# A hybrid SSM and short-convolution layer: other parameter loads and transposes, an earlier scaling in the opening, and another order of the last tiles

## The chip, the cores and the metric

One Trainium2 chip, of which the kernel uses one core. The metric is the device time of one execution in microseconds; the kernel before took 429.47 us (median of three runs, 429.3 to 429.89).

## The reference

One decoder layer for 1024 tokens of width 1024, all in fp32. The input is normalised and projected to six parts of 512 columns; an S5 state-space mixer takes one of them, a gated convolution three, and a SiLU gate path has one for each mixer.

```python
def reference(x, norm_gain, w_in, ...):
    h = x
    xn = rmsnorm(h, norm_gain[l])                       # 1024 x 1024
    proj = jnp.einsum('bld,dc->blc', xn, w_in[l])       # 1024 x 3072
    # u_ssm, z_ssm, h_conv, b_conv, c_conv, z_conv: 512 columns each
    y_ssm = s5_mixer(u_ssm, ...) * jax.nn.silu(z_ssm)
    y_conv = short_conv_mixer(h_conv, b_conv, c_conv, conv_w[l]) * jax.nn.silu(z_conv)
    y = jnp.concatenate([y_ssm, y_conv], axis=-1)
    h = h + jnp.einsum('blc,cd->bld', y, w_out[l])
    return rmsnorm(h, final_norm_gain)

def s5_mixer(u, a_re, a_im, log_dt, b_re, b_im, c_re, c_im, d_skip, w_glu, b_glu):
    # 32 groups of 16 channels, 64 complex states each
    # a, dt -> discretised ab (exp, sin, cos); bb = q * b
    # s = scan over positions of s = ab * s + bb u;  y = Re(c s) + d u
    # y = gelu(y); y = y * sigmoid(y @ w_glu + b_glu)
```

In the reference b_re and b_im have the shape (group 32, state 64, channel 16), c_re and c_im (group 32, channel 16, state 64).

## The kernel before

Tokens are held as eight tiles of 128 rows, tile `i` with the tokens 8c + i. Each tile is normalised, transposed on PE (`turn`, tiles `ps_x`), and scaled by the gain into a high part `xh` in fp32r (`gain`, on ACT) and a low part `xl` (`rest`, on DVE). Every projection is the sum of three products, high by high, high by low and low by high, of 8 matmuls each, into one of the four PSUM banks of the pool `pmm`; `psm` has the other four.

The opening has its order on PE, ACT and DVE written out by hand, in the string `START` (line 33), under `tc.manual_schedule`. A word of it stands for a step: `s`, `n` are square and norm of a tile, `t`, `g`, `x` the transposes, `xh` and `xl` of a pair of tiles (0 to 3), `w` warming transposes, `W` and `L` the high and low parts of the weights. `u` and `U` are products of the SSM input: digits for blocks and then the quarter of the tokens, then which of the three products; `u` takes the blocks one after the other, `U` alternates between them. `k20` (`keep_u`) is ACT's copy of block 2, half 0, from PSUM to the tile `us`, which has two buffers, and four transfers of it to the scratch tensor `uscr` on SP's queue. `p0` to `p2` are `transpose_params`, `d` with a number so many steps of `discretise`, the DVE computation of the SSM parameters, and `C` three ACT copies that lay `craw` into `cb`.

In `cb`, rows 0 to 31 hold C by group (through `craw` and `C`), rows 32 to 63 B by group, loaded directly. `p1` and `p2` transpose it channel by channel, 32 transposes of 64x64 in four tiles `ps_cb`, and ACT lays the results out as `b1`, `b2`, `c1`, `c2` of 128 rows (state, real and imaginary) by 512 (group, channel).

All loads are issued on SP's queue, in program order in the opening: x, w, the small parameters, x again, then C and B, then the transfers of `uscr`.

After the opening the scheduler places the steps of the string `ORDER`: convolution blocks (`mm_h`, `mm_c`, `mm_b`, `mm_z`) with the SSM's steps between them (`ssm_prep` makes `vv`, `rr` and `ec` on DVE; `ssm_lags` multiplies `vv` in `ps_k`). Then come the GLU, the gate products `mm_zs`, and the output product as seven products of half-size operands for each of four pairs of row tiles. A pair has the accumulators `ow`, `oz`, `ox`; DVE adds them to the residual tiles `xr` (`xa` and `xb` for a pair), ACT takes squares with a sum (`sq`), and the root of the final norm is computed on DVE alone by an integer estimate and three Newton steps (`rsqrt_steps`, lines 88 to 99). In the last pair the last of the seven products is made in two halves of 256 columns, and GpSimd multiplies by the gain ahead of the root.

Of the kernel before, what the change touches and what calls it, by code (L numbers as in the profile page):

```python
# [30 lines left out]
EPS = 1e-6  # L31
WARM = (26, 8, 14)
START = ("s0 w0 n0 c s1 W0 n1 W1 w1 t0 L0 g0 L1 U010hl x0 u010x. W2 s2 s3 W3 L2 n23 u20hx u30hx t1 L3 g1 u230l. s4 x1 s5 n45 "
         "U01231h u01lx. k00 p0 u11lx. k10 t2 u21lx. k20 u31lx. k30 d12 g2 s6 x2 s7 C n67 d12 U01232h u01232l t3 g3 d8 x3 u01232x. "
         "U01233h u03l p1 p2 u03x. k01 u13lx. k11 d u23lx. k21 u33lx. k31")
ORDER = "p0 0 1 2 m0 q0 i0 3 p1 4 5 o0 6 m1 q1 i1 7 p2 8 o1 9 m2 q2 i2 10 p3 11 o2 m3 q3 i3 12 13 o3 14 15"
MAGIC = 12582912.0
# [20 lines left out]
def hybrid_kernel(ctx: ExitStack, tc, x, norm_gain, w_in, a_re, a_im, log_dt, b_re, b_im,  # L58
# [68 lines left out]
    par = tc.alloc_tile_pool(name="par", bufs=1)  # L127
    xpool = tc.alloc_tile_pool(name="xstage", bufs=8)

    cb = big.tile([2 * NG, 3 * S * H], F32, tag="cy", name="cb")  # L130
    cb = cb.rearrange("g (r p h) -> g r p h", h=H, r=3)
    craw = pst.tile([NG, 2, H, S], F32, name="craw")
    lam_r = pst.tile([NG, 2, 2, S], F32, name="lam_r")
    ldt = pst.tile([P, NG], F32, name="ldt")
    d_r = pst.tile([NG, H], F32, name="d_r")
# [34 lines left out]
    nc.sync.dma_start(rows, conv_w[0].rearrange("k (b p) -> (k b) p", p=P))  # L170
    nc.sync.dma_start(rowb, b_glu[0].rearrange("(b p) -> b p", p=P))
    load((4, 5, 6, 7))
    nc.sync.dma_start(craw[:, 0], c_re[0])
    nc.sync.dma_start(craw[:, 1], c_im[0])
    for k, src in enumerate((b_re, b_im, b_re)):
        nc.sync.dma_start(cb[NG:2 * NG, k], src[0])


    pw = pmm.tile([P, P], F32, tag="mm", name="ps_warm")
# [69 lines left out]
    lam = par.tile([P, 2, NG], F32, name="lam")  # L249
    c1 = par.tile([P, NG, H], F32, name="c1")  # L250
    c2 = par.tile([P, NG, H], F32, name="c2")
    b1 = pst.tile([P, NG, H], F32, name="b1")
    b2 = pst.tile([P, NG, H], F32, name="b2")
    dT = par.tile([H, NG], F32, name="dT")

    def transpose_params(part):
        if part == 0:
            ps = psm.tile([P, 2, NG], F32, tag="sm", name="ps_lam")
            for k in range(2):
                PE.transpose(ps[:, k], lam_r[:, k].rearrange("g d p -> g (d p)"), ident[0:NG, 0:NG])  # L260
            A.copy(lam, ps)
            ps = psm.tile([P, 16 + NG], F32, tag="sm", name="ps_rows")
            PE.transpose(ps[:, 0:12], rows, ident[0:12, 0:12])
            PE.transpose(ps[:, 12:16], rowb, ident[0:NB, 0:NB])
            PE.transpose(ps[0:H, 16:16 + NG], d_r, ident[0:NG, 0:NG])
            A.copy(cw, ps[:, 0:12])
            A.copy(bg, ps[:, 12:16])
            A.copy(dT, ps[0:H, 16:16 + NG])
            return
        off = part - 1  # L270
        for q in range(2):
            hs = slice(q * 8, q * 8 + 8)
            ps = psm.tile([P, 8, 2 * NG], F32, tag="sm", name=f"ps_cb{off}{q}")
            for h in range(8):
                PE.transpose(ps[:, h], cb[:, off:off + 2, :, 8 * q + h].rearrange("g r p -> g (r p)"), ident[0:2 * NG, 0:2 * NG])  # L275
# [146 lines left out]
    with tc.manual_schedule(engines={mybir.EngineType.PE, mybir.EngineType.Activation, mybir.EngineType.DVE}):  # L424
        for what in START.split():
# [4 lines left out]
                warm(WARM[n[0]])  # L430
            elif what[0] == "d":
                discretise(int(what[1:]) if what[1:] else None)
            elif what[0] == "C":
                for k in range(3):
                    A.copy(cb[0:NG, k], craw[:, k % 2].rearrange("g h p -> g p h"))
# [381 lines left out]
    def mult(ps, op_a, op_b, j, first, cols=slice(0, 512)):  # L817
        out_ = ps[:, 0:cols.stop - cols.start]
        for m, (p, q) in enumerate(((0, 0), (0, 1), (1, 0))):
            for k in range(NB):  # L820
                PE.matmul(out_, aq[op_a, j][:, p, k], bq[op_b, k][:, q, cols], start=first and m + k == 0,  # L821
                          stop=m == 2 and k == NB - 1, skip_group_check=True)
# [16 lines left out]
    def finish(j, m, parts):  # L839
# [4 lines left out]
        V.scalar_tensor_tensor(x, x, r, g2b, MUL, MUL)  # L844
        nc.sync.dma_start(out_ci[:, 2 * j + m, :], x)

    load_res(0)
    first_product(0)
    for j in pairs:
# [32 lines left out]
        Q.tensor_tensor(ga[:, hi_], xa[:, hi_], g2b[:, hi_], MUL)  # L882
        Q.tensor_tensor(gb[:, hi_], xb[:, hi_], g2b[:, hi_], MUL)
        Q.tensor_tensor(ga[:, lo_], xa[:, lo_], g2b[:, lo_], MUL)
        ops, r = rsqrt_steps([part[:, 0:1], part[:, 1:2]])
        for op in ops:
            op()
        A.activation(xa, ga, AF.Copy, scale=r)
        nc.sync.dma_start(out_ci[:, 2 * j, :], xa)
        steps, r = rsqrt_steps([part[:, 2:3], part[:, 3:4], part[:, 4:5]])  # L890
        for q in range(2):
            c = slice(q * 256, q * 256 + 256)
            mult(pw[j][:, c], "A22", "T4", j, False, c)
            add(xb[:, c], pw[j][:, c])
            final_square(xb[:, c], part[:, 3 + q:4 + q])
            Q.tensor_tensor(gb[:, c], xb[:, c], g2b[:, c], MUL)
# [4 lines left out]
        A.activation(xb[:, hi_], gb[:, hi_], AF.Copy, scale=r)
        for c in (lo_, hi_):
            nc.sync.dma_start(out_ci[:, 2 * j + 1, c], xb[:, c])
    ph3.release()
# [30 lines left out]
```

## Time and profile before

| what | value |
|---|---|
| median of three runs | 429.47 us (429.3, 429.89, 429.47) |
| profiled execution | 429.41 us, span 427.5 us, mean granted TensorE clock 0.990 |
| PE busy | 414.7 us, 97% of the span, 2226 instructions |
| DVE busy | 333.3 us, 78% |
| ACT busy | 183.5 us, 43% |
| transfers on SP's queue | 47712 packets, 45.42 MB |

The span runs from the first to the last instruction, and the execution is 1.9 us longer. PE is the engine that matmuls and transposes run on, PEld its weight loads, DVE the vector engine, ACT the scalar engine, POOL GpSimd, SP the queue that issues most transfers. "L230" is a line of the kernel. A row of the chain gives a start, a duration, and the work that the end of the program was waiting for at that time.

### The profile page before, as it was taken

What the parts mean: (1) busy time and instruction counts of PE and PEld (TensorE: products, weight loads), DVE (VectorE), ACT (ScalarE), POOL (GpSimd) and SP (SyncE); (2) the same over time, 40 slices, a digit from 0 to 9 for tenths busy, and PEclk for the clock granted to TensorE, in tenths of its full rate; (3) what the DMA queues carried; (4) which work ended last, traced back from release to release, by engine and by line L of the source; (5) the groups of instructions that cost most, each with busy time, mean ns of one, the idle gap of its engine ahead of it and who ended that gap; (6) DMA issues with size and microseconds to landing.
All of it is one profiled execution on the core that took longest, in us unless ns stands there. A gap on an engine that the chain in (4) does not pass through costs nothing.

```text
span 427.5 us, 6316 instructions
## 1 busy us (share of the span) xinstructions
PE 414.7 (97%) x2226; PEld 355.2 (83%) x2226; DVE 333.3 (78%) x820; ACT 183.5 (43%) x331; POOL 36.5 (9%) x41
## 2 busy tenths in 40 slices
PE   8898999999999999999999999999999999999992
PEld 7898999888888888888888888888888888888881
DVE  4973898969998999997997934867186799978634
ACT  4743944143423346135324413647335664333113
POOL 0000003000120020200022000120112100000022
PEclk9999998999999999999999999999999999999997
DMA  7892104514080361355025431677554550333212
GB/s 228 242 288 69 32 2 117 179 43 155 13 207 7 113 184 46 80 136 162 0 52 126 134 90 53 195 196 208 138 147 74 141 130 1 106 115 126 98 50 99
DMA packets 49472, 48.96 MB, mean 115 GB/s; under 512 B 6697, under 2 KB 39489, under 8 KB 49441
## 3 DMA queue, kind: packets, MB, share of 16 engines
q1 hardware_dynamic: 47712, 45.42, 35.7%
q0 software_dynamic: 1728, 3.15, 4.3%
q8 instruction: 17, 0.28, 0.3%
q14 instruction: 15, 0.11, 0.1%
HBM read 31.65 MB, written 8.39 MB: 94 GB/s over the span
## 4 chain that ended last, share of the span: by engine, by line
PE 94%; DMA 2%; DVE 1%; ACT 1%; issue 1%; SPq 1%; ACTq 0%
PE mm_u L230 11%; PE mm_b L230 10%; PE mm_c L230 10%; PE mm_h L230 10%; PE mm_z L230 10%; PE mm_zs L230 10%; PE ow L821 10%; PE glu L749 5%; PE oz L821 5%; PE ox L821 3%; DMA wru<-in_w_in_dram 2%; PE ps_s L571 2%; PE ps_y L595 2%; PE ps_y L596 2%; PE ps_x L211 1%; PE ps_cb L275 1%
## 5 line engine op out<-in xcount | busy, mean ns | idle before, releaser
L643 POOL TENSOR_TENSOR cy<-cy,sg 128x512 f32<-128x512 f32 x8 | 16.1, 2015 | 179.2 <-DVE sg L642 146.9
L828 ACT ACTIVATE sq<-xr 128x512 f32<-128x512 f32 (+1 forms) x17 | 10.3, 605 | 38.7 <-DVE xr L825 27.2
L749 PE MATMUL glu<-shl,wg 128*128 128x512 f32 x96 | 21.9, 389 | 0.0
L749 PEld LDWEIGHTS glu<-shl,wg 128*128 128x128 f32 x96 | 18.0, 188 | 3.7
L224 DVE SCALAR_TENSOR_TENSOR xl<-ps_x,g,xh 128x256 fp32r<-128x256 f32 x32 | 12.9, 476 | 8.6 <-ACT xh L218 8.6
L230 PE MATMUL mm_u<-xh,whu 128*128 128x256 f32 x128 | 17.5, 288 | 1.8 <-ACT xh L218 1.8
L230 PE MATMUL mm_u<-xh,wlu 128*128 128x256 f32 x128 | 18.6, 292 | 0.0
L230 PE MATMUL mm_u<-xl,whu 128*128 128x256 f32 x128 | 18.3, 293 | 0.0
L230 PEld LDWEIGHTS mm_u<-xh,whu 128*128 128x128 f32 x128 | 16.2, 191 | 2.5 <-ACT xh L218 2.2
L821 PE MATMUL ow<-bs,ax 128*128 128x512 f32 (+1 forms) x54 | 16.9, 367 | 0.5 <-DVE xr L825 0.5
L230 PEld LDWEIGHTS mm_u<-xh,wlu 128*128 128x128 f32 x128 | 17.1, 200 | 0.1
L230 PEld LDWEIGHTS mm_u<-xl,whu 128*128 128x128 f32 x128 | 17.0, 200 | 0.1
L230 PE MATMUL mm_b<-xh,whb 128*128 128x512 f32 x64 | 16.4, 398 | 0.0
L230 PE MATMUL mm_c<-xh,whc 128*128 128x512 f32 x64 | 16.1, 391 | 0.0
L230 PE MATMUL mm_h<-xh,whh 128*128 128x512 f32 x64 | 16.1, 391 | 0.0
L230 PE MATMUL mm_h<-xh,wlh 128*128 128x512 f32 x64 | 16.1, 390 | 0.0
L230 PE MATMUL mm_b<-xh,wlb 128*128 128x512 f32 x64 | 15.9, 391 | 0.0
L230 PE MATMUL mm_b<-xl,whb 128*128 128x512 f32 x64 | 15.8, 390 | 0.0
L230 PE MATMUL mm_h<-xl,whh 128*128 128x512 f32 x64 | 15.8, 389 | 0.0
L230 PE MATMUL mm_z<-xh,wlz 128*128 128x512 f32 x64 | 15.8, 389 | 0.0
L230 PE MATMUL mm_zs<-xh,whzs 128*128 128x512 f32 x64 | 15.8, 389 | 0.0
L230 PE MATMUL mm_zs<-xl,whzs 128*128 128x512 f32 x64 | 15.8, 389 | 0.0
(354 smaller groups left out, 1106.5 us busy)
## 6 DMA issues: line engine op xcount, KB each, us to landing
ee<-ec SPq DMA_DIRECT2D x16, 256.0 KB
wro<-in_w_out_dram SPq DMA_DIRECT2D x8, 512.0 KB
xr<-in_x_dram SPq DMA_DIRECT2D x8, 512.0 KB
out_dram<-xr SPq DMA_DIRECT2D x7, 512.0 KB
x<-in_x_dram SPq DMA_DIRECT2D x6, 512.0 KB
wrh<-in_w_in_dram SPq DMA_DIRECT2D x4, 512.0 KB
wrc<-in_w_in_dram SPq DMA_DIRECT2D x4, 512.0 KB
uscr<-us SPq DMA_DIRECT2D x32, 64.0 KB
```

The costliest lines, as they stand in the source:

```text
L211: PE.transpose(pss[kt // 2][:, kt % 2, j], x_t[2 * pair + j][:, kt * P:(kt + 1) * P], ident)
L224: V.scalar_tensor_tensor(xl[pair // 2][:, kt, n], ps, g1[:, kt:kt + 1], hs.bitcast(F32), MUL, SUB)
L230: PE.matmul(ps[:, n], a[:, kt], b[half][:, kt, n], start=what == "h" and kt == 0, stop=last and kt == KT - 1)
L275: PE.transpose(ps[:, h], cb[:, off:off + 2, :, 8 * q + h].rearrange("g r p -> g (r p)"), ident[0:2 * NG, 0:2 * NG])
L571: PE.matmul(ps[:, g - 4 * q], w1[:, g], u2[:, g], start=True, stop=True)
L595: PE.matmul(ps[:, k], tp[:, g], u2[:, g], start=True, stop=False)
L596: PE.matmul(ps[:, k, 1:C], vv[:, g, 1:T + 1].rearrange("p t h -> p (t h)"), xa[:, g, 0:C - 1], start=False, stop=True)
L643: Q.tensor_tensor(yb[:, n], yb[:, n], sg, MUL)
L749: PE.matmul(ps, wg[:, a, k, es], shl[half][:, y, k], start=m + k == 0, stop=m == 2 and k == NB - 1)
L821: PE.matmul(out_, aq[op_a, j][:, p, k], bq[op_b, k][:, q, cols], start=first and m + k == 0, stop=m == 2 and k == NB - 1, skip_group_check ...
L828: A.activation(temp(f"sq{final_square.n}")[:, 0:x.shape[-1]], x, AF.Square, accum_out=acc)
```

## The change

Four things change.

1. C is loaded three times (real, imaginary, real) in blocks of 128 rows (8 groups by 16 channels), so that 8 transposes of 128x128 in two tiles `ps_c` replace the 32. B goes from its tensor straight into `b1` and `b2`, by four transfers whose runs are the 16 channels of a group and state. The step `C` is gone; one ACT operation turns the signs of half of `b2`.
2. In `START`, `g2` stands ahead of `k20`, and the product `U01232h` of four blocks is split into `U012h`, blocks 0 and 1, and `U232h`, blocks 2 and 3.
3. The second half of the last product has a PSUM bank of its own, `ol`, and the order of the last pair's steps on ACT and DVE is written out by hand. The residual takes the part of the second half that is already in `ow` by an extra addition. The whole root of `xa` stands ahead of the last addition on DVE.
4. The root of `xb` is ACT's Sqrt, DVE's reciprocal and one Newton step. A Sqrt of one column of a scratch tile ahead of the first output product loads its table. The scaling of `xa` is split between DVE and ACT.

```diff
-START: ... k10 t2 u21lx. k20 u31lx. k30 d12 g2 s6 x2 s7 C n67 d12 U01232h u01232l t3 g3 d8 x3 u01232x. ...
+START: ... k10 t2 g2 u21lx. k20 u31lx. k30 d12 s6 x2 s7 n67 d12 U012h U232h u01232l t3 g3 d8 x3 u01232x. ...
...
-    nc.sync.dma_start(craw[:, 0], c_re[0])
-    nc.sync.dma_start(craw[:, 1], c_im[0])
-    for k, src in enumerate((b_re, b_im, b_re)):
-        nc.sync.dma_start(cb[NG:2 * NG, k], src[0])
+    for k, src in enumerate((c_re, c_im, c_re)):
+        nc.sync.dma_start(craw[:, :, k], src[0].rearrange("(b g) h p -> (g h) b p", g=G))
+    b1 = pst.tile([P, NG, H], F32, name="b1")
+    b2 = pst.tile([P, NG, H], F32, name="b2")
+    for dst, srcs in ((b1, (b_re, b_im)), (b2, (b_im, b_re))):
+        for k, src in enumerate(srcs):
+            nc.sync.dma_start(dst[k * S:k * S + S], src[0].rearrange("g p h -> p g h"))
...
-        for q in range(2):
-            hs = slice(q * 8, q * 8 + 8)
-            ps = psm.tile([P, 8, 2 * NG], F32, tag="sm", name=f"ps_cb{off}{q}")
-            for h in range(8):
-                PE.transpose(ps[:, h], cb[:, off:off + 2, :, 8 * q + h].rearrange("g r p -> g (r p)"), ident[0:2 * NG, 0:2 * NG])
-            for dst, lo, scale in (...):
-                A.activation(dst[:, :, hs], ps[:, :, lo:lo + NG].rearrange("p h g -> p g h"), AF.Copy, scale=scale)
+        ps = psm.tile([P, NB, P], F32, tag="sm", name=f"ps_c{off}")
+        for b in range(NB):
+            PE.transpose(ps[:, b], craw[:, b, off:off + 2].rearrange("q r p -> q (r p)"), ident)
+        dst, scale = ((c1, sgn), (c2, -1.0))[off]
+        A.activation(dst.rearrange("p (b g) h -> p b (g h)", b=NB), ps, AF.Copy, scale=scale)
+        if off:
+            A.activation(b2, b2, AF.Copy, scale=nsgn)
...
-            elif what[0] == "C":
-                for k in range(3):
-                    A.copy(cb[0:NG, k], craw[:, k % 2].rearrange("g h p -> g p h"))
...
+    A.activation(temp("root")[:, 0:1], ident[:, 0:1], AF.Sqrt)
     load_res(0)
     first_product(0)
...
-        ops, r = rsqrt_steps([part[:, 0:1], part[:, 1:2]])
-        for op in ops:
-            op()
-        A.activation(xa, ga, AF.Copy, scale=r)
+        ops, ra = rsqrt_steps([part[:, 0:1], part[:, 1:2]])
+        vh, v2, rb, t = (const.tile([P, 1], F32, name=f"last_{m}") for m in ("vh", "v2", "rb", "t"))
+        pl = psm.tile([P, 512], F32, tag="sm", name="ol")
+        with tc.manual_schedule(engines={mybir.EngineType.Activation, mybir.EngineType.DVE}):
+            add(xb[:, 256:512], pw[j][:, 256:512])
+            for q in range(2):
+                c = slice(q * 256, q * 256 + 256)
+                bank = pl if q else pw[j][:, c]
+                mult(bank, "A22", "T4", j, q == 1, c)
+                add(xb[:, c], bank[:, 0:256])
+                final_square(xb[:, c], part[:, 3 + q:4 + q])
+                Q.tensor_tensor(gb[:, c], xb[:, c], g2b[:, c], MUL)
+                if q == 0:
+                    for op in ops:
+                        op()
+                    V.tensor_scalar(vh, part[:, 2:3], 0.5 / D, 0.5 * EPS, MUL, ADD)
+                    V.scalar_tensor_tensor(vh, part[:, 3:4], 0.5 / D, vh, MUL, ADD)
+                    V.tensor_scalar(v2, vh, 2.0, None, MUL)
+            A.activation(t, part[:, 4:5], AF.Sqrt, scale=1.0 / D, bias=v2)
+            V.tensor_scalar_mul(xa[:, lo_], ga[:, lo_], ra)
+            V.scalar_tensor_tensor(vh, part[:, 4:5], 0.5 / D, vh, MUL, ADD)
+            A.activation(xa[:, hi_], ga[:, hi_], AF.Copy, scale=ra)
+            V.reciprocal(rb, t)
+            V.scalar_tensor_tensor(v2, rb, vh, rb, MUL, MUL)
+            V.scalar_tensor_tensor(rb, v2, 1.5, rb, SUB, MUL, reverse0=True)
+            V.tensor_scalar_mul(xb[:, lo_], gb[:, lo_], rb)
+            A.activation(xb[:, hi_], gb[:, hi_], AF.Copy, scale=rb)
         nc.sync.dma_start(out_ci[:, 2 * j, :], xa)
-        steps, r = rsqrt_steps([part[:, 2:3], part[:, 3:4], part[:, 4:5]])
-        for q in range(2):
...
-            steps.pop(0)()
-        for step_ in steps:
-            step_()
-        V.tensor_scalar_mul(xb[:, lo_], gb[:, lo_], r)
-        A.activation(xb[:, hi_], gb[:, hi_], AF.Copy, scale=r)
```

ACT in the opening, before, from k10's copy on (`mm_u` of a copy is the block's bank, `ps_x` the transposes of a pair, `x` a tile):

```order
L243 COPY us_596<-mm_u_306 128x512
L243 COPY us_638<-mm_u_400 128x512
L243 COPY us_660<-mm_u_417 128x512
L218 ACTIVATE xh_85<-ps_x_602,g_111 128x256 x2
L218 ACTIVATE xh_85<-ps_x_603,g_111 128x256 x2
L218 ACTIVATE xh_85<-ps_x_604,g_111 128x256 x2
L218 ACTIVATE xh_85<-ps_x_605,g_111 128x256 x2
L192 ACTIVATE ysb,ss_686<-x_118 128x1024
L192 ACTIVATE ysb,ss_696<-x_119 128x1024
L435 COPY cb<-craw 32x1024 x3
L218 ACTIVATE xh_85<-ps_x_805,g_111 128x256 x2
```

And after:

```order
L244 COPY us_597<-mm_u_307 128x512
L219 ACTIVATE xh_85<-ps_x_603,g_110 128x256 x2
L219 ACTIVATE xh_85<-ps_x_604,g_110 128x256 x2
L219 ACTIVATE xh_85<-ps_x_605,g_110 128x256 x2
L219 ACTIVATE xh_85<-ps_x_606,g_110 128x256 x2
L244 COPY us_647<-mm_u_401 128x512
L244 COPY us_669<-mm_u_418 128x512
L193 ACTIVATE ysb,ss_687<-x_117 128x1024
L193 ACTIVATE ysb,ss_697<-x_118 128x1024
L219 ACTIVATE xh_85<-ps_x_803,g_110 128x256 x2
```

The eight scalings of the third pair now stand ahead of the copies of blocks 2 and 3, and the fourth pair's follow the squares at once.

SP's queue after, from the last load of x to the second group of `uscr` transfers (before, five loads of 32x1024 stand in the place of the seven):

```order
L146 DMA x_118<-in_x_dram 128x1024
L172 DMA craw<-in_ssm_c_re_dram 128x4x64
L172 DMA craw<-in_ssm_c_im_dram 128x4x64
L172 DMA craw<-in_ssm_c_re_dram 128x4x64
L177 DMA b_147<-in_ssm_b_re_dram 64x32x16
L177 DMA b_147<-in_ssm_b_im_dram 64x32x16
L177 DMA b_148<-in_ssm_b_im_dram 64x32x16
L177 DMA b_148<-in_ssm_b_re_dram 64x32x16
L246 DMA uscr<-us_564 8x16x128 x4
L246 DMA uscr<-us_597 8x16x128 x4
```

The seven loads stand ahead of every transfer that empties a buffer of `us`.

DVE at the end after, from the last addition of a whole bank on (`xr_3719` is xa, `xr_3721` xb, `ssp` the sums of squares, `y_3951` the root of xa; the rows of the second and third Newton step are cut):

```order
L821 TENSOR_TENSOR xr_3719<-xr_3719,ox_3875 128x512
L821 TENSOR_TENSOR xr_3721<-xr_3721,ow_3830 128x256
L92 TENSOR_SCALAR vh_3950<-ssp_3873 128x1
L94 SCALAR_TENSOR_TENSOR vh_3950<-ssp_3873,vh_3950 128x1
L95 TENSOR_SCALAR y_3951<-vh_3950 128x1
...
L899 TENSOR_SCALAR last_v_3954<-last_vh 128x1
L821 TENSOR_TENSOR xr_3721<-xr_3721,ol 128x256
L902 TENSOR_SCALAR xr_3719<-ysb,y_3951 128x512
L903 SCALAR_TENSOR_TENSOR last_vh<-ssp_3873,last_vh 128x1
L905 RECIPROCAL last_rb<-last_t 128x1
```

Before, the last addition from `ow` stands behind eight of the root's steps of xa and one of xb's, and eight steps of xb's root follow it.

More of the change, by code (lines that the diff above doesn't have):

```diff
@@ L33 @@
 START = ("s0 w0 n0 c s1 W0 n1 W1 w1 t0 L0 g0 L1 U010hl x0 u010x. W2 s2 s3 W3 L2 n23 u20hx u30hx t1 L3 g1 u230l. s4 x1 s5 n45 "
-         "U01231h u01lx. k00 p0 u11lx. k10 t2 u21lx. k20 u31lx. k30 d12 g2 s6 x2 s7 C n67 d12 U01232h u01232l t3 g3 d8 x3 u01232x. "
+         "U01231h u01lx. k00 p0 u11lx. k10 t2 g2 u21lx. k20 u31lx. k30 d12 s6 x2 s7 n67 d12 U012h U232h u01232l t3 g3 d8 x3 u01232x. "
          "U01233h u03l p1 p2 u03x. k01 u13lx. k11 d u23lx. k21 u33lx. k31")
@@ L128, in hybrid_kernel @@
     xpool = tc.alloc_tile_pool(name="xstage", bufs=8)
-    cb = big.tile([2 * NG, 3 * S * H], F32, tag="cy", name="cb")
-    cb = cb.rearrange("g (r p h) -> g r p h", h=H, r=3)
-    craw = pst.tile([NG, 2, H, S], F32, name="craw")
+    craw = pst.tile([P, NB, 3, S], F32, name="craw")
     lam_r = pst.tile([NG, 2, 2, S], F32, name="lam_r")
@@ L251, in hybrid_kernel @@
     c2 = par.tile([P, NG, H], F32, name="c2")
-    b1 = pst.tile([P, NG, H], F32, name="b1")
-    b2 = pst.tile([P, NG, H], F32, name="b2")
     dT = par.tile([H, NG], F32, name="dT")
@@ L270, in transpose_params @@
         off = part - 1
-        for q in range(2):
-            hs = slice(q * 8, q * 8 + 8)
-            ps = psm.tile([P, 8, 2 * NG], F32, tag="sm", name=f"ps_cb{off}{q}")
-            for h in range(8):
-                PE.transpose(ps[:, h], cb[:, off:off + 2, :, 8 * q + h].rearrange("g r p -> g (r p)"), ident[0:2 * NG, 0:2 * NG])
-            for dst, lo, scale in ((b2 if off else b1, NG, nsgn if off else 1.0), (c2 if off else c1, 0, -1.0 if off else sgn)):
-                A.activation(dst[:, :, hs], ps[:, :, lo:lo + NG].rearrange("p h g -> p g h"), AF.Copy, scale=scale)
+        ps = psm.tile([P, NB, P], F32, tag="sm", name=f"ps_c{off}")
[5 more added lines that the diff above has]
+            A.activation(b2, b2, AF.Copy, scale=nsgn)
     steps = []
@@ L884, in hybrid_kernel @@
         Q.tensor_tensor(ga[:, lo_], xa[:, lo_], g2b[:, lo_], MUL)
-        ops, r = rsqrt_steps([part[:, 0:1], part[:, 1:2]])
-        for op in ops:
-            op()
-        A.activation(xa, ga, AF.Copy, scale=r)
-        nc.sync.dma_start(out_ci[:, 2 * j, :], xa)
-        steps, r = rsqrt_steps([part[:, 2:3], part[:, 3:4], part[:, 4:5]])
-        for q in range(2):
[L892 to L896, printed above, removed]
-            steps.pop(0)()
```

## The prediction

> **What bounds the kernel now.** I read the busy table and the chain of work on the page first, since they say which engine a saving must come from.
>
> ```profile
> PE 414.7 (97%) x2226; PEld 355.2 (83%) x2226; DVE 333.3 (78%) x820; ACT 183.5 (43%) x331; POOL 36.5 (9%) x41
> PE 94%; DMA 2%; DVE 1%; ACT 1%; issue 1%; SPq 1%; ACTq 0%
> ```
>
> PE holds 94% of the chain, so an edit pays only where PE loses instructions, clock or a wait, or behind PE's last product. The waits of PE tell how much idle time there is to win.
>
> ```profile
> PE mm_u L230 <- ACT xh L218: 1.8, 2, 1.1
> PE ow L821 <- DVE xr L825: 0.5, 1, 0.5
> ```
>
> Next the chain in order of time (start, us, what), for the places that the change touches.
>
> ```profile
> 35.23 1.75 PE ps_x L211 x16
> ...
> 40.88 0.58 ACT us L243
> ...
> 41.90 7.94 PE mm_u L230 x64
> ...
> 51.59 8.63 PE mm_u L230 x72
> 60.22 3.66 PE ps_cb L275 x32
> 63.88 8.41 PE mm_u L230 x56
> 72.29 5.47 PE mm_h L230 x24
> ```
>
> Between 40.9 and 41.9 the chain leaves PE for ACT. The parameter transposes ps_cb take 3.66 us, and the 56 products behind them take 8.41 us, or 0.150 each, where the 72 ahead took 8.63, or 0.120. The stretches (columns: busy us, then the granted clock, DMA share, GB/s) say why:
>
> ```profile
> 63.00:64.00 1.00, 1.00 (x9) 0.93 (x9) 0.86 (x6) 0.83 (x3) 0.00 (x0) 0.93 0.00 0
> 64.00:65.00 1.00, 1.00 (x5) 1.00 (x6) 0.83 (x6) 0.67 (x2) 0.00 (x0) 0.50 0.00 0
> ...
> 67.00:68.00 1.00, 1.00 (x9) 1.00 (x9) 1.00 (x1) 0.44 (x1) 0.00 (x0) 0.86 0.00 0
> ```
>
> PE was granted half its clock from just before 64 to past 67, right behind ps_cb.
>
> **The opening, part by part.** *Transposes.* 32 transposes of 64x128 become 8 of 128x128. A 128x128 transpose takes 1.75/16 = 0.109 us in the ps_x row, so 8 take 0.88: **-2.78 us**, all on PE's path.
>
> *Clock.* The 56 products at 0.120 would take 6.72: the slow stretch cost 1.69. The 16 transposes of ps_x at 35.23 (1.75 us) show no such loss behind them, 0.120 per product. The new block of 0.88 is half of that block, so I take the drop as gone: **-1.69**; kept, it is worth 0.
>
> *The third pair's high parts.* In the timeline, with ACT's wait order:
>
> ```profile
> 41.37 3.03 ACT L218 ACTIVATE xh<-ps_x,g 128x256 fp32r<-128x256 f32 x8
> 41.90 4.10 PE L230 MATMUL mm_u<-xh,whu 128*128 128x256 f32 x32 [1.09 <-ACT xh L218]
> 46.52 5.95 ACT L435 COPY cb<-craw 32x1024 f32<-32x1024 f32 x3
> 33.38 11.11 SPq L245 DMA_DIRECT2D uscr<-us  x16
> ```
>
> The eight scalings start only when k30's copy has been made, and that waits for block 3's last product at 40.88. Put ahead of k20, they start behind ps_x (end 36.98) and take 3.03: ready by about 40.1, before PE's 40.81. k20 then runs at about 40.1 to 40.7 and k30 at 40.9 to 41.5. Blocks 2 and 3 of the next product need the banks that these two free; PE gets there after 16 products of 0.120, at 42.8, so 1.3 us are spare. **-1.09**.
>
> ACT loses the three C copies (5.95), and its eight parameter evictions become two of 128x512 and a scaling of b2; it is idle over half the time, so this pays only through what ACT hands to DVE.
>
> *Loads.* Five loads of 32 rows become three of 128x4 runs of 256 B (1536 packets) and four of 64x32 runs of 64 B, 8192 packets in all, or 512 for each of 16 DMA engines. They sit in SP's queue between x and the uscr writes of `us`. `us` has two buffers, so k20 waits until k00's four writes have landed, k30 for k10's. The loads begin where the five begin now, near 28:
>
> ```profile
> 26.00:28.00 2.00, 2.00 (x19) 2.00 (x18) 2.00 (x6) 2.00 (x6) 0.00 (x0) 1.00 1.11 406
> 28.00:30.00 2.00, 2.00 (x19) 2.00 (x18) 0.97 (x7) 1.66 (x4) 0.00 (x0) 1.00 1.01 197
> 36.00:40.00 4.00, 4.00 (x36) 4.00 (x35) 0.00 (x0) 0.59 (x1) 0.00 (x0) 1.00 0.37 98
> 17.50:17.75 0.25, 0.25 (x4) 0.25 (x3) 0.25 (x1) 0.25 (x1) 0.00 (x0) 1.00 0.23 45
> q1 hardware_dynamic: 47712, 45.42, 35.7%
> ```
>
> No row has 64-B reads alone. Bounds per packet and engine: low, the 128-B load of log_dt at 17.5: 45 GB/s for 0.25 us are 88 packets, 0.23 x 0.25 us on 16 engines, 10 ns. High, the mean of the queue, 35.7% of 16 x 427.5 us over 47712 packets of 952 B: 51 ns. Between them, w's 512-B runs at 406 GB/s (20 ns) and the uscr writes of 512 B (98 GB/s at share 0.37: 31 ns). I take 15: these are reads like w's, with an eighth of the bytes, so nearest to the 128-B row. With 96 packets of C (2 us) the loads end at 30 + 7.7 = 37.7; k00's and k10's writes (64 packets at 31 ns, 2 us) end by 39.7, and with some 1.5 us to land (an estimate from the tail row below: data until 426, end 427.5) k10's are there by 41.2, k30's 40.9 nearly kept. **0**, up to about 17 ns; each further ns costs 0.5 us.
>
> The Trainium skill, "DMA: Bandwidth & Descriptors", Specifications, speaks against this edit: transfers under 512 B are read, modified and written. By that rule a 64-B packet would cost no less than a 512-B one, and the sum would lose the 0 for what the rival below has. The 128-B row at 10 ns contradicts it so far.
>
> Sum to the end of the opening: -2.78 - 1.69 - 1.09 = **-5.56**.
>
> **What is late next: DVE.** DVE computes the SSM parameters beside PE's convolution blocks, and rows of the timeline and the chain show how close it is:
>
> ```profile
> 52.37 2.95 ACT L218 ACTIVATE xh<-ps_x,g 128x256 fp32r<-128x256 f32 x8
> 66.98 1.23 DVE L106 TENSOR_TENSOR wlh<-wrh,whh 128x1024 fp32r<-128x1024 f32 x1 [0.77 <-ACT whh L105]
> 77.44 1.23 DVE L106 TENSOR_TENSOR wlz<-wrz,whz 128x1024 fp32r<-128x1024 f32 x1 [0.59 <-ACT whz L105]
> 88.86 0.92 ACT L288 ACTIVATE rotc<-rot 64x112 f32<-64x112 f32 x3 [10.48 <-DVE rot L288]
> 95.50 0.68 DVE L620 TENSOR_TENSOR vp<-hs,mm_c 128x512 f32<-128x512 f32 x1
> 103.76 1.35 DVE L505 TENSOR_TENSOR vv<-vv,tv 128x1152 f32<-128x1152 f32 x1
> 105.83 0.32 PE ps_k L546 x2
> 95.00:105.00 10.00, 10.00 (x46) 8.23 (x46) 9.96 (x13) 2.44 (x3) 0.00 (x0) 1.00 0.63 193
> ```
>
> vv ends at 105.11, 0.7 before ps_k reads it, and DVE is busy 9.96 of 10 us there. DVE's chain starts earlier too, but not by 5.56. Its gate is the fourth pair's high parts, which start at 52.37, when the C copies (46.52 + 5.95) are done. Without the copies PE's transposes set that start: they end at 51.59 now, 50.5 when 1.09 earlier, and the scalings begin on their first banks, near 49.4: 3.0 sooner. DVE has some 0.6 of its own steps to do first, so 2.4; its waits on weight casts further on (0.77 and 0.59 in the rows) go too, as ACT has the casts ready earlier: 3.7 in all, an estimate, so that rot's end at 88.9 moves to about 85. vv is then ready at 101.4, PE at 100.2: **+1.2** given back. Bounds: 0 (DVE gains enough) and +2.5 (it gains 2.4 and no more).
>
> **The root's table.** Sqrt on a scratch column between the casts at 343 to 346 adds one table load, 1.28 us by its row, and a column's operation on ACT. Casts there run back to back at 0.52 each; PE's first product needs the first of them only, ACT gets the rest back within the first pair. **0**; with no cover, +1.3 once. Behind it only squares, copies and Sqrt follow.
>
> ```profile
> 97.71 1.28 ACT L641 ACT_TABLE_LOAD   x1
> ```
>
> **The tail.**
>
> ```profile
> 417.31 0.42 DVE xr L825
> ...
> 419.90 0.24 ACT xr L888
> ...
> 420.95 0.50 ACT sq L828 x2
> 421.48 0.17 DVE vh L94
> ...
> 423.21 0.72 ACT xr L901
> 423.80 0.81 SPq L903 DMA_DIRECT2D out_dram<-xr  x2
> 425.00:426.00 1.00, 0.00 (x0) 0.00 (x0) 0.00 (x0) 0.00 (x0) 0.00 (x0) 0.50 0.99 381
> ```
>
> The second half of the last product no longer waits for DVE's read of the bank: PE ends 0.5 earlier, about 418.9. But DVE now does all nine root steps of xa and three more ahead of the last add; at 0.216 each (the eight from 421.48 to 423.21 are 1.73) plus independence, they end near 420.1, 0.45 later than now. The square no longer stands behind xa's scaling of 1.15 us, so it ends near 421.1, 0.4 earlier. Then one Sqrt (about 0.3), reciprocal (0.3) and two steps (0.43) replace eight: scales at 422.2 instead of 423.2. xa's scaling, however, now stands behind the Sqrt on ACT and ahead of xb's: xa's transfer is issued near 422.2, not 421.1, and the three outputs of 1 MB run together. 512 KB take 1.35 us at 381 GB/s: 0.8 from issue to data (423.8 to 424.6), 2.7 of data, 1.5 to land: 427.15. **-0.35**; bounds 0.9 worse (the table must be loaded here: 1.28 - 0.35) and 1.2 better (outputs not serial).
>
> **Sum:** -5.56 + 1.2 - 0.35 = -4.7. The profiled execution took 429.41 (span 427.5, 1.9 around it), 0.06 under the median of 429.47; the forecast is **424.8**. Of the likeliest case alone the range is 423.3 to 426.0.
>
> **Rivals.**
>
> *B's loads hold up k20 (the other side).* If a 64-B packet takes 24 ns or more, the loads end at 30 + 12.3 or later, k10's writes have landed 3.5 after that, k30's copy ends near 46.4 and PE, due at 42.8, stalls some 3.5 in the split product; at 31 ns the loads end at 45.9, the stall is 7.1: -4.7 + 7.1 = +2.4, and an idle stretch of that length may bring another 1.69 of half clock: 432 to 434. At 51 ns it is 442. It decides from about 26 ns (the 4.7 gone). For it: the uscr row's 31. Against: 10 ns for 128 B. The skill's page named above gives this rival; its rule as a mechanism (a read before each write, two passes at 20 ns) means 40 ns, 512 x 40 = 20.5, loads end at 50.5: 437. Chance 0.15 in all, 0.04 of it for 40 ns and more.
>
> *Part of this stall,* 17 to 24 ns, costing 0.5 to 3.5: 425.3 to 428.5. Chance 0.17.
>
> *DVE keeps more:* its chain moves 2.4 only and the SSM blocks run at DVE's pace: -5.56 + 2.5 - 0.35 = -3.4, 426.1. For it: 9.96 of 10 busy. Against: the waits of PE name DVE nowhere in that stage. Chance 0.13.
>
> *DVE keeps nothing and the tail pays:* -5.56 - 0.35 to -1.2: 422.7 to 423.5. Chance 0.12.
>
> *The clock drop stays* (it was some other thing than the length of the transposes): -3.0, 426.4. Chance 0.07.
>
> **How the numbers follow.** The forecast's case has 0.36. 0.2% (0.86 us) is about what a measurement tells from no change. Slower: the first rival's upper part, 0.15; same: its threshold and the partial stall's end, 0.06; faster: 0.79. Leaving out some 0.14 above and 0.06 below, the range is 423.0 to 429.3.
>
> **What would show it.** ps_c at 0.88 and clock 1.00 behind it; no wait of PE on xh near 41; k20's copy at about 40, or named as waiting on a transfer; a wait of PE at ps_k on vv of about 1; three output transfers issued within 1.2 us. A wait of PE at the split product, or DMA share high past 40, makes the forecast wrong.

## The result and the profile after

The changed kernel took 426.81 us (median of six runs, 425.42 to 427.51), the kernel before 429.28 in the same comparison: ratio 0.9949, 95% interval 0.9932 to 0.9966, or 2.5 us of gain. The forecast was 424.8, 4.7 us of gain, almost twice what came. The direction held, and the wide range of 423.0 to 429.3; the range of the likeliest case, 423.3 to 426.0, did not. Against the larger sets of the kernel before that stand beside the experiments (429.17, 428.57 and 429.04) the gain is 1.8 to 2.4 us. One execution of the kernel before in the first of these sets took 697.69 us at a granted clock of 0.557, and the ratios leave it out.

The profiled execution has a span of 424.7 us, against 427.5. The page's busy table and chain:

```profile
PE 410.9 (97%) x2202; PEld 350.8 (83%) x2202; DVE 334.7 (79%) x819; ACT 177.6 (42%) x326; POOL 35.8 (8%) x41
PE 80%; DVE 11%; ACT 2%; DMA 2%; issue 2%; SPq 1%; ACTq 0%; DVEq 0%
```

PE has 3.8 us less to do, and its share of the chain fell from 94% to 80%: DVE now carries 11% of it. The waits of PE say the same. The wait of 0.5 at the end is gone, as is one of the two on xh; four new ones are there; the wait on xh that is left is the first product's.

```profile
PE ps_k L542 <- DVE vv L501: 0.8, 1, 0.8
PE mm_c L231 <- DVE vp L616: 0.7, 1, 0.7
PE mm_u L231 <- ACT xh L219: 0.7, 1, 0.7
PE mm_b L231 <- ACT us L244: 0.6, 1, 0.6
PE mm_u L231 <- ACT us L244: 0.4, 1, 0.4
```

A ledger by place needs a common zero. The first product of the opening starts once the first x has been loaded and scaled, at 12.1 to 13.0 us in the profiles of this study, in no order that goes with the edit, so every time below is counted from it. These are PE's rows of the timeline for the kernel before (start, duration, the first matmul, the first of mm_h, of ps_k, of the output product):

```profile
12.98 1.23 PE L230 MATMUL mm_u<-xh,whu 128*128 128x256 f32 x6 [0.71 <-ACT xh L218]
72.12 2.00 PE L230 MATMUL mm_h<-xh,whh 128*128 128x512 f32 x8
105.76 0.39 PE L546 MATMUL ps_k<-vv,bb 128*16 128x128 f32 x2
342.12 0.39 PE L821 MATMUL ow<-bd,bs 128*128 128x512 f32 x1
```

and for the changed kernel:

```profile
12.38 1.84 PE L231 MATMUL mm_u<-xh,whu 128*128 128x256 f32 x9 [0.67 <-ACT xh L219]
66.33 2.00 PE L231 MATMUL mm_h<-xh,whh 128*128 128x512 f32 x8
102.70 0.39 PE L542 MATMUL ps_k<-vv,bb 128*16 128x128 f32 x2 [0.76 <-DVE vv L501]
339.37 0.39 PE L817 MATMUL ow<-bd,bs 128*128 128x512 f32 x1
```

| from the first product to | before | after | difference |
|---|---|---|---|
| mm_h (end of the opening) | 59.14 | 53.95 | -5.19 |
| ps_k | 92.78 | 90.32 | -2.46 |
| the output product | 329.14 | 326.99 | -2.15 |
| the end of the span | 414.52 | 412.32 | -2.20 |

The opening gained 5.2 us. Of these, 2.7 were given back on the 36 us up to ps_k and 0.3 more between ps_k and the output product; the piece from the first output product to the end, all four pairs and the tail, took 85.33 instead of 85.38. The 0.60 by which the first product came earlier is the rest of the difference in span.

Why DVE is late shows in ACT's timeline of the changed kernel (copies k20 and k30, the squares s6 and s7) and in DVE's first step behind the first square:

```profile
39.69 0.58 ACT L244 COPY us<-mm_u 128x512 f32<-128x512 f32 x1 [0.88 <-DMA uscr<-us]
42.00 0.58 ACT L244 COPY us<-mm_u 128x512 f32<-128x512 f32 x1 [1.72 <-DMA uscr<-us]
42.48 1.06 ACT L193 ACTIVATE ysb<-x 128x1024 f32<-128x1024 f32 x1
43.66 1.06 ACT L193 ACTIVATE ysb<-x 128x1024 f32<-128x1024 f32 x1
43.66 0.15 DVE L92 TENSOR_SCALAR vh<-ss 128x1 f32<-128x1 f32 x1 [3.78 <-ACT ysb L193]
```

ACT stands still for 1.72 us ahead of k30 until the uscr transfers have landed. The squares of the last two tiles stand behind it on ACT, the norm of those tiles on DVE behind the squares, and the steps of discretise behind the norm; DVE idles 3.78 us. SP's queue tells what held the transfers:

```profile
24.70 1.44 SPq L172 DMA_DIRECT2D craw<-in_ssm_c_re_dram  x1
26.19 0.74 SPq L177 DMA_DIRECT2D b<-in_ssm_b_re_dram  x1
26.97 6.08 SPq L177 DMA_DIRECT2D b<-in_ssm_b_im_dram  x2
33.10 1.31 SPq L177 DMA_DIRECT2D b<-in_ssm_b_re_dram  x1
34.50 10.71 SPq L246 DMA_DIRECT2D uscr<-us  x16
```

The four loads of B hold SP from 26.19 to 34.41, and the first uscr transfer, whose data were ready at 32.8, is issued at 34.50, 1.7 late. In the kernel before, the last load of B was this one, and the first uscr transfer was issued at 33.38, when its data were ready:

```profile
24.75 0.42 SPq L176 DMA_DIRECT2D cb<-in_ssm_b_re_dram  x1
```

### The profile page after: what moved, and what is told of

Same layout as the page of the kernel before. It is cut to its first block, busy times and chain, and to the rows that moved or that the text cites. A ratio compares the mean times of both kernels' runs of the same rounds, so it can differ in the third digit from the quotient of the medians.

```text
span 424.7 us, 6263 instructions
## 1 busy us (share of the span) xinstructions
PE 410.9 (97%) x2202; PEld 350.8 (83%) x2202; DVE 334.7 (79%) x819; ACT 177.6 (42%) x326; POOL 35.8 (8%) x41
## 4 chain that ended last, share of the span: by engine, by line
PE 80%; DVE 11%; ACT 2%; DMA 2%; issue 2%; SPq 1%; ACTq 0%; DVEq 0%
PE mm_zs L231 10%; PE ow L817 10%; PE mm_b L231 9%; PE mm_z L231 9%; PE mm_c L231 8%; PE mm_h L231 8%; PE mm_u L231 6%; PE oz L817 5%; PE glu L745 5%; PE ox L817 3%; DVE e L287 2%; PE ps_s L567 2%; DMA wru<-in_w_in_dram 2%; PE ps_y L591 2%; PE ps_y L592 2%
## 5 line engine op out<-in xcount | busy, mean ns | idle before, releaser
L639 POOL TENSOR_TENSOR cy<-cy,sg 128x512 f32<-128x512 f32 x8 | 15.2, 1904 | 180.3 <-DVE sg L638 180.3
L219 ACT ACTIVATE xh<-ps_x,g 128x256 fp32r<-128x256 f32 x32 | 12.1, 489 | 8.9 <-PE ps_x L212 8.9
L231 PE MATMUL mm_c<-xl,whc 128*128 128x512 f32 x64 | 15.8, 389 | 0.0
```

Of the source, the lines that this page charges most:

```text
L219: A.activation(xh[pair // 2][:, kt, n], ps, AF.Copy, scale=g1[:, kt:kt + 1])
L231: PE.matmul(ps[:, n], a[:, kt], b[half][:, kt, n], start=what == "h" and kt == 0, stop=last and kt == KT - 1)
L639: Q.tensor_tensor(yb[:, n], yb[:, n], sg, MUL)
```

## The experiments

Theory A: the missing gain was lost on DVE, because B's loads hold SP's queue, that holds k20 and k30, and these hold the squares and DVE's whole chain. Its main rival is the prediction's own account, in which the fourth pair's high parts set DVE's time. The first four kernels ran beside one set of runs of the kernel before (median 429.17), the next four beside another (428.57), the last four beside a third (429.04).

**Four buffers of us.**

```diff
-        us = xw.tile([P, 4, C], F32, tag="us", name=f"us{b}{half}", bufs=2)
+        us = xw.tile([P, 4, C], F32, tag="us", name=f"us{b}{half}", bufs=4)
```

> The tile us has four buffers instead of two, so ACT's copies k20 and k30 wait for no transfer of uscr; the loads of B stay where they are. Theory A (the missing gain was lost because B's loads hold SP's queue, which holds k20 and k30, and with them the squares s6, s7 behind them on ACT and the whole DVE chain): k30 ends near 40.8 instead of 42.6, the squares end 1.7 us earlier, DVE's chain at vv moves by about 1.7, PE's wait in the split product (0.4) goes and its three waits on vp, us and vv (2.0 in all) shrink to under 0.7; total 1.3 to 2.0 us below the changed kernel's 426.8, so 424.8 to 425.5. Rival B (DVE's chain is bound by the fourth pair's high parts and its own work, as the prediction had it): only the 0.4 goes, and DVE gives it back; total 426.4 to 426.8, waits on vp, us and vv unchanged or larger.

425.89 us, ratio 0.9929 (0.9913 to 0.9945); 0.9 below the changed kernel, less than theory A said and more than the rival. The place is as theory A had it:

```profile
39.98 0.59 ACT L244 COPY us<-mm_u 128x512 f32<-128x512 f32 x1 [0.98 <-PE mm_u L231]
41.65 0.15 DVE L92 TENSOR_SCALAR vh<-ss 128x1 f32<-128x1 f32 x1 [2.06 <-ACT ysb L193]
99.31 1.35 DVE L501 TENSOR_TENSOR vv<-vv,tv 128x1152 f32<-128x1152 f32 x1
```

k30 now waits for PE alone. Counted from the first product, vv's last step starts at 87.22 instead of 88.92 (101.30 - 12.38), and ps_k at 88.62 instead of 90.32: 1.70 each. The wait at ps_k stays at 0.8, since PE came earlier too. Of the 1.70, 1.2 were left at the output product, where a wait of 0.4 of mm_zs on ACT (`sgl`) was new in this execution, and the piece from there to the end took 86.00 instead of 85.33.

This profile also tells the two gates apart. The page's chain of the changed kernel leads to DVE through the fourth pair's high parts, as the rival has it:

```profile
49.66 1.94 ACT xh L219 x5
```

But DVE's timeline has no idle time ahead of the low parts that follow them. With four buffers the high parts start only 0.62 earlier (36.66 instead of 37.28 after the first product), DVE's step behind the second square 1.73 earlier (30.74 instead of 32.47), and vv moved with the squares. One thing is not as firm: in the six profiles with two buffers and B's loads ahead of the transfers (the changed kernel and five below) k30 starts 28.58 to 30.12 after the first product, against 27.89 here, so the 1.7 stands for 0.7 to 2.2.

**B's loads behind the transfers.** A copy of one column from `us` (by GpSimd, into b1 and b2, overwritten by the loads) makes the four loads wait for k30.

```diff
-START: ... k30 d12 s6 ...
+START: ... k30 b d12 s6 ...
...
+            elif what[0] == "b":
+                for t in (b1, b2):
+                    Q.tensor_copy(t[:, 0, 0:1], kept[:, 0, 0:1])
+                load_b()
```

> The four loads of B wait for k30's copy (a copy of one column by GpSimd from us into b1 and b2 ahead of them), so they stand behind the uscr transfers of the first half in SP's queue; us keeps two buffers. Theory A: the first uscr transfer is issued near 32.8 instead of 34.5, k30 ends near 41, the squares and DVE's chain come about 1.5 us earlier; total 425.0 to 425.7. Rival B: nothing but PE's 0.4, total 426.4 to 426.8. Rival C (the loads cost by their data on the 16 engines, wherever they stand): they now hold up the copies of the second half instead, and the total stays at 426.5 or more.

425.52 us, ratio 0.9921 (0.9904 to 0.9938). The first uscr transfer is issued at 32.93, k30 starts 27.95 after the first product instead of 29.62, vv's last step 1.62 earlier. Two independent ways to free k30 move DVE's chain by the same 1.6 to 1.7, and the total is 1.3 below the changed kernel with the same data loaded, so the rival that counts their data falls. This run also has B's loads alone on the queue:

```profile
46.00:48.00 2.00, 2.00 (x20) 2.00 (x19) 1.79 (x12) 0.00 (x0) 0.00 (x0) 1.00 0.90 88
48.00:50.00 2.00, 2.00 (x21) 2.00 (x20) 1.69 (x10) 0.83 (x3) 0.00 (x0) 1.00 1.04 100
50.00:52.00 2.00, 2.00 (x19) 2.00 (x18) 2.00 (x6) 2.00 (x7) 0.00 (x0) 1.00 0.90 74
```

(88 + 100 + 74) GB/s for 2 us each are 524 KB, the 8192 packets of 64 B, in about 6 us. With 512 of them on each of 16 engines, that is 6000/512 = 12 ns for a packet, and 11 by the busy share.

**DVE's idle time filled.**

```diff
-k30 d12 s6 x2 s7 n67 d12 U012h U232h u01232l t3 g3 d8 x3
+k30 d12 s6 x2 d16 s7 n67 d12 U012h U232h u01232l t3 g3 d16 x3
```

> Sixteen of the discretise steps stand on DVE between the third pair's low parts and the norm of the last two tiles, and eight more ahead of the fourth pair's low parts; nothing else. DVE is idle for 3.8 us there in the changed kernel, waiting for the squares. Theory A in its wider form (what PE lost again is DVE's chain, and DVE's chain is late by idle time at the squares): DVE's vv moves by 2.5 to 3.5 us, PE's waits on vp, us and vv go to under 0.5; total 424.6 to 425.3. Rival D (the waits come from the transfers and copies on ACT, not from DVE's work): vv moves, PE's wait on us stays, total within 0.4 of 426.8.

424.66 us, ratio 0.9904 (0.9887 to 0.9921), and PE waits for DVE only 0.6 at vp. The same copies wait for the same transfers; DVE just has work meanwhile. But the gain is not all from the filled 3.5 us: vv's last step starts 6.8 us earlier (94.80 - 12.64 = 82.16). The scheduler places what follows the opening, and with rot ready earlier it put `rr` and the first step of `vv` ahead of the cast part `wlc` instead of behind it. In the changed kernel DVE waits there, with vv queued behind:

```profile
88.10 1.23 DVE L106 TENSOR_TENSOR wlh<-wrh,whh 128x1024 fp32r<-128x1024 f32 x1 [1.65 <-ACT whh L105]
91.89 1.23 DVE L106 TENSOR_TENSOR wlc<-wrc,whc 128x1024 fp32r<-128x1024 f32 x1 [2.56 <-ACT whc L105]
```

So theory A has a second half: idle time of DVE in a fixed order. By place the 6.8 divides into 4.2 up to the end of rot (69.83 instead of 74.07 after the first product, 0.6 of it because a step of `vp` moved behind rot) and 2.5 behind it. What the filled idle time gave and what the new order gave, this run does not tell apart.

**The old tail.** The last pair as before, and no early Sqrt (the diff of the change, undone for that part).

> The changed kernel with the last pair as before (one bank, DVE's root for both, one scaling of xa on ACT, no early Sqrt). Reading of the two traces: from the first matmul of the last product to the end the changed kernel is only about 0.05 us shorter, so the tail is worth nothing: total within 0.3 us of 426.8. The prediction's term was 0.35, which would make this 427.2. If the tail had gained 1 us that the traces hide, 427.8.

426.36 us, ratio 0.9948 (0.993 to 0.9967), the same ratio as with the new tail. From the output product to the end it takes 426.2 - 340.90 = 85.30, against 85.33. In all, that piece took 85.30 to 85.55 in the six profiles with the old tail (the kernel before three times, this one, and the two that follow) and 85.33 to 86.23 in the six with the new tail as it is: the tail, its bank, its order, its root and its table load together, gained nothing that these runs can tell.

**C and B alone.** The kernel before with the loads and transposes of the change, without `C`; START's order and the tail as before.

> The kernel before with the change to C and B alone (loads, transposes, no step C); START's order, the tail and the root as before. Theory A (DVE's chain is gated by the squares s6 and s7 on ACT, which stand behind k20, k30 and here also behind the third pair's high parts, and k20 and k30 wait for uscr transfers that B's loads hold up): k30 ends about 1.7 us later than before, the high parts and squares with it, PE's wait on xh near 41 grows from 1.1 to 2 or more, DVE's vv comes later than before, and PE gives all its 4.5 us back at vp, us and vv; total 0.5 to 2 us above the kernel before, 429.7 to 431. The prediction's terms would give -2.8 - 1.7 and 1.2 back: 426. Rival B with only PE's own wait: 426.5 to 427.5.

427.54 us, ratio 0.9976 (0.9957 to 0.9994): faster by 1.0, where theory A had it slower and the prediction's terms 3 us faster. Half of theory A came: PE's wait on xh grew from 1.1 to 2.5, and the squares ended 1.4 later (35.07 after the first product, before 33.64). The product in the timeline:

```profile
42.86 5.58 PE L231 MATMUL mm_u<-xh,whu 128*128 128x256 f32 x32 [2.52 <-ACT xh L219]
```

The stretches beside it (columns as in the prediction's):

```profile
44.00:45.00 1.00, 1.00 (x7) 1.00 (x7) 1.00 (x4) 1.00 (x4) 0.00 (x0) 0.50 0.41 105
```

The 32 products took 5.58 instead of 4.10 us, at half clock: one slow stretch was removed and another came. It may not come each time. The twelve executions fall into six with a mean clock of 0.994 or more, 425.94 to 427.07 us, and six with less, 428.00 to 430.19; the profiled one, 428.00 at 0.992, is of the second group. So the median of 427.54 stands for neither, and without the half clock this edit may be worth the 2.1 us that the first group (median 426.51) has; no profile of that group is there to show it. The half that failed is DVE's: its chain regained the 1.4 and 0.7 more before vv, with 4.4 us of waits on the casts of both blocks' weights instead of 5.9, so its gate is not the squares alone.

**The third pair's high parts alone.** The kernel before with g2 ahead of k20 and the product in two halves.

> The kernel before with the third pair's high parts ahead of k20 and k30 and the product in two halves of blocks; C, B and the tail as before. Theory A: k20 and k30 keep their time (nothing holds the uscr transfers), PE's 1.1 us wait goes, the squares come 3 us earlier, C's copies hide, so DVE is not later than PE; PE keeps all of 1.1: 427.9 to 428.3 against 429.2 before. The prediction has the same 1.1. Rival: the copies k20 and k30 wait for their transfers all the same and PE waits 0.3 or more in the split product: 428.5 or more.

428.09 us, ratio 0.9989 (0.9972 to 1.0007): unclear, 0.5 of the 1.1 expected. PE's wait on xh is gone and there is none in the split product. But the scheduler's order changed here too, and PE waits 1.1 at ps_s for a copy that ACT makes late:

```profile
PE ps_s L571 <- ACT ysb L532: 1.1, 1, 1.1
```

**xa's scaling ahead of the last square.** The added line stands behind `v2` in the branch for the first half, the removed one stood behind the Sqrt.

```diff
+                    A.activation(xa[:, hi_], ga[:, hi_], AF.Copy, scale=ra)
...
-            A.activation(xa[:, hi_], ga[:, hi_], AF.Copy, scale=ra)
```

> The changed kernel with ACT's scaling of xa's high half ahead of the last square instead of behind the Sqrt; nothing else. Theory T (the end is set by the first of the three output transfers: 1 MB in a row from xa's issue on): xa is issued near 418.8 instead of 419.9 in the frame of the changed kernel, the span from the last product's end to the end shrinks by 0.7 to 1.1 us; total 425.7 to 426.1. Rival U (the end is set by the issue of the last transfer, xb's high half): the last square is not delayed, the last issue stays, and the total stays at 426.8; if the square is delayed by the scaling, up to 0.3 more.

426.83 us, ratio 0.9946 (0.9925 to 0.9967): no change in the median, where theory T had 0.7 to 1.1 of gain. In the trace the piece from the output product to the end is 84.64 instead of 85.33, with xa's transfer issued 1.1 earlier and the last two where they were, as theory T has it. The profiled execution, the slowest of the six at 427.84, also had 1.1 of wait at mm_zs, where the other profiles have 0 to 0.5. A gain of 0.7 is not to be read from these medians, and the case for it is the trace alone.

**More transposes.** 24 more 128x128 transposes behind ps_c.

```diff
+        if off:
+            for n in range(24):
+                PE.transpose(ps[:, n % NB], craw[:, n % NB, off:off + 2].rearrange("q r p -> q (r p)"), ident)
```

> The changed kernel with 24 more 128x128 transposes behind the eight of ps_c (3.5 us of transposes in a row instead of 0.9, as long as the 3.7 us of the kernel before); they write the same places again. If the half clock behind ps_cb came from the length of the stretch of transposes, PEclk shows 0.50 for about 3.4 us in the stretch that begins near the end of these transposes, and the products there take 0.15 us and more each. If it came from something else (64-row operands, the evictions, chance), PEclk stays 1.00 and only 2.6 us are added on PE.

One execution, 427.18 us. PEclk is 1.00 up to the tail, so in this profile 3.4 us of transposes in a row (58.40 to 61.81) were followed by no half clock. And PE, with 2.5 us more to do, comes to ps_k at 89.99 after the first product (102.64 - 12.65), no later than the changed kernel (90.32), without a wait there. That fits PE having time to spare up to ps_k, but does not show it: the order behind rot changed here as in the filled kernel, and vv's last step starts 4.0 earlier.

**The kernel before, twice more,** to see whether the half clock recurs.

> The kernel before, unchanged, for a second look at PEclk behind ps_cb. If the half clock there belongs to the stretch of transposes, PEclk is 0.50 for 3.4 us near 64 again. If it comes in some executions only (the kernel with the third pair's high parts moved kept ps_cb and showed 1.00 throughout; 24 more transposes in the changed kernel showed 1.00 too), it is absent here or stands at another place, and the first matmul of mm_h comes 1.5 to 1.8 us earlier after the first mm_u than the 59.1 us of the first profile.

> The kernel before, unchanged, a third look; the same two readings as for the second.

It recurs in both (428.89 us). In the first of the two profiles it lasts from 63.0 to 66.4:

```profile
62.00:63.00 1.00, 1.00 (x11) 1.00 (x11) 0.84 (x5) 0.86 (x3) 0.00 (x0) 1.00 0.00 0
63.00:64.00 1.00, 1.00 (x7) 0.89 (x7) 0.86 (x6) 0.81 (x3) 0.00 (x0) 0.50 0.00 0
66.00:67.00 1.00, 1.00 (x9) 1.00 (x8) 0.28 (x1) 1.00 (x2) 0.00 (x0) 0.80 0.00 0
```

Three profiles of the kernel before have it, from 3.2 to 3.7 us behind the start of ps_cb on; the kernel with g2 alone has the same ps_cb for 3.73 us and none. So it goes with ps_cb, but not always. Whether the placing decides or the single execution, one profile cannot say, and the mean clocks speak for the execution: the three profiled ones have 0.989 or 0.990, and of the 54 other executions of the kernel before beside these runs 32 have 0.991 or less (median 429.1 us) and 22 more (median 428.2). If these 22 had no half clock, the 1.69 is a gain over part of the executions only; none of them was profiled. In the profiles of kernels with the new transposes there is no half clock behind them.

**Casts later.** The weights of the second convolution block at normal priority, so that ACT makes rotc and the copies of us first.

```diff
-        with tc.high_priority():
+        with (ExitStack() if nm in ("h1", "c1") else tc.high_priority()):
```

> The changed kernel with the loads and casts of the second convolution block's weights (wrh, wrc, whh, whc of block 1) at normal priority, so that ACT makes all six rotc copies and the copies of us before the cast whh, which stood between them. Theory E (part of DVE's lateness is its fixed order behind rot: it waits 1.6 and 2.6 us for the casts whh and whc, with rr and vv queued behind): PE's wait on us (0.6) goes, vv comes 1 to 2 us earlier against the first matmul, PE's wait at ps_k (0.8) goes to under 0.3; total 425.6 to 426.1. Rival (only the squares gate the chain): total 426.6 to 427.0, waits as in the changed kernel.

427.95 us, ratio 0.9971 (0.9957 to 0.9986): slower than the changed kernel by the medians. ps_k came 0.8 earlier (89.49 after the first product) and the wait of mm_b on us went, as expected, but a wait of 1.9 came next:

```profile
PE ps_s L567 <- ACT ysb L528: 1.9, 1, 1.9
```

ACT's copy of ps_w stands behind a scaling that waits for DVE, a table load and a sigmoid. What one order gave, the next wait took.

**The best version.** The filled idle time, four buffers of us, and xa's scaling ahead of the last square, together.

> The changed kernel with three edits at once: sixteen discretise steps in DVE's idle time before the last two tiles' norm and eight more ahead of the fourth pair's low parts, four buffers of us, and ACT's scaling of xa's high half ahead of the last square. Theory A: the first gave 424.7 alone; the second takes PE's 0.4 in the split product away; the third shortens the end by 0.7 in its trace: 423.4 to 424.2. Rival (edits in the opening compete for one limit, and the end's 0.7 is lost to the transfers as its median said): 424.4 to 424.8.

423.01 us (422.74 to 423.11), ratio 0.986 (0.9845 to 0.9874): 6.0 us below the kernel before and 3.8 below the changed one, the fastest of the study and lower than theory A said. PE's waits behind the opening are gone, and DVE's at the squares is 0.2:

```profile
PE ps_x L212 <- DVE x L204: 1.1, 2, 1.0
PE mm_u L231 <- ACT xh L219: 0.7, 1, 0.7
DVE vh L92 <- ACT ysb L193: 0.2, 1, 0.2
```

ps_k stands at 86.98 after the first product (before 92.78): the 5.2 to 5.8 us of the opening are kept whole once DVE keeps up.

## Why the prediction was right or wrong

- **PE's opening, -5.56: right in the profile.** 5.19 came, and the 0.36 to it is the wait in the split product. The transposes took 0.79 from start to next start (0.88 forecast), the clock stayed at 1.00 behind them, and the 1.09 on xh went. The reason given for the clock, the length of the stretch of transposes, was not shown: 3.4 us of 128x128 ones were followed by no half clock, and in the kernel before it seems to be missing from part of the executions. That the 1.69 came whole in this pair of profiles may be luck in part.
- **B's loads at 0: size right, consequence wrong.** The packet was put at 15 ns and measured 12, so the loads did not reach the rival's 24. The Trainium skill, "DMA: Bandwidth & Descriptors", Specifications, says that transfers under 512 B miss the line rate because they are read, modified and written. They do miss it here, with 74 to 100 GB/s where a row of before has 406; what the prediction made of it, that a 64-B packet cannot cost less than a 512-B one, does not hold at 12 ns. The 20 ns that stood for w's 512-B runs are a doubtful reading: from 19 to 26 us, ahead of that row, 2.5 MB moved, and the two loads of w ahead of x in the queue have 1.05 MB, so the row is probably x's runs of 4 KB. Where one of w's later loads is in flight, 81 to 82 in the trace of before, 272 GB/s at a share of 0.95 give 29 ns. But only the data of B's loads were counted. SP's own issue of them took 8.2 us, where five loads took 0.4 each before, and the transfers of uscr started 1.7 late behind them. So k30, put at 40.9, started 1.72 later after the first product than before (29.62, before 27.90). "Nearly kept" was priced by PE's 1.3 us of slack alone: PE lost 0.36 by it, but the squares behind k30 on ACT had no slack.
- **DVE's 3.7 and the 1.2 given back: the step that failed.** DVE's vv moved by 1.86 (90.78 to 88.92 after the first product), not 3.7, so PE gave back 2.7, not 1.2. Of the 3.7, 2.4 were to come ahead of the fourth pair's low parts and 1.3 at the casts behind; 1.20 came there and 0.66 behind. The estimate took the fourth pair's high parts as DVE's gate. In the trace of before DVE was busy all the way from the norm of the last tiles to the low parts (the first two rows below; no idle time stands at the second), so its gate was the squares, and k30 in front of them; and the prediction had k30 nearly in time. With k30 freed in two ways, 1.6 to 1.7 of the missing 1.8 came back, and vv then stands 3.5 to 3.6 earlier than before: nearly the size that was forecast, by another gate than was named, so the size alone proves nothing for the estimate. Even then PE gives back 1.6 of an opening of 5.8 (four buffers of us: ps_k 4.16 earlier). The rest of what PE could keep lay in idle time of DVE's fixed order, at the squares and at the casts whh and whc; the casts' waits (1.84 and 2.38, the last two rows) stood in the trace of before, and the row that was quoted, 9.96 busy of 10, began just behind them.

```profile
46.65 0.16 DVE L92 TENSOR_SCALAR vh<-ss 128x1 f32<-128x1 f32 x1 [1.03 <-ACT ysb L192]
53.45 3.22 DVE L224 SCALAR_TENSOR_TENSOR xl<-ps_x,g,xh 128x256 fp32r<-128x256 f32 x8
90.75 1.23 DVE L106 TENSOR_TENSOR wlh<-wrh,whh 128x1024 fp32r<-128x1024 f32 x1 [1.84 <-ACT whh L105]
94.35 1.23 DVE L106 TENSOR_TENSOR wlc<-wrc,whc 128x1024 fp32r<-128x1024 f32 x1 [2.38 <-ACT whc L105]
```

- **The tail, -0.35: nothing.** Counted from the output product, PE's end came 0.8 earlier (0.5 forecast), but the add behind twelve small steps came 1.0 us later than before (0.45 forecast; one step that ran beside ACT's square took 0.74, where the same step took 0.15 to 0.29 before), and xb's scales came 0.5 earlier instead of 1.0. The end came 0.05 earlier. That the three transfers in a row took the rest fits the 84.64 with xa's transfer issued earlier, and 84.77 in the best version, two profiles. Undoing the whole part changed no more than the interval.
- **The table load at 0:** right as far as shown; the run without it has the same ratio.
- **The rivals.** "DVE keeps more", 426.1 at a chance of 0.13, comes nearest: the SSM blocks ran at DVE's pace, and the time is 0.7 off. But its condition was 2.4 of DVE's chain at the high parts; what came was 1.9, held back by the transfers behind B's loads, the place that the first rival named and priced by data alone. The sign that the prediction set against itself, a wait of PE at the split product, came: 0.36.

## What to carry to other kernels

When the bounding engine is made faster, the price of every later wait is read from the next engine's chain, and its gate is found by walking back through its in-order queue to the first idle stretch, not to the nearest operand. An added wait costs the whole queue behind it: here the wait ahead of k30 cost PE 0.36 us and DVE 1.7, through the two squares behind it. Idle time of an in-order engine ahead of its critical work can be filled by hand, and of the single edits to the changed kernel that paid most (2.2 us by the medians, against 0.9 and 1.3 for freeing k30); but where a scheduler sets the order behind the edit, a single run cannot say which of the two paid.

## What the runs showed of the hardware

64-B reads of B took 12 ns each on an engine, two fifths of the 31 ns of 512-B writes to uscr. Two of their loads together held SP for 6.08 us in the changed kernel and for 2.53 us where they stand behind the transfers (issued at 45.24), where a load of 32 rows held it 0.42. The half clock lasted 3.4 us in each of the four profiles that have it in the opening: three of the kernel before, and the one with C and B alone, where it began 0.8 us after PE had resumed from 2.5 us of idle time, 3.3 us after that idle time began. Why the 3.7 us of 64-row transposes bring it in three profiles and not in a fourth, and 3.4 us of 128-row ones not at all in one, stays open, and so does the wait of 0 to 1.1 us at mm_zs that comes and goes between executions.
